# Gating groups taken in pairs, ten feed-forward chunks tile by tile, and norm and mixer steps issued by an account of product time and vector time

## The chip, the cores and the metric

One core of one Trainium2 chip runs the whole kernel. The metric is the device time in microseconds (us) of one execution; the kernel before has a median of 2253.11 us over three runs (2252.66 to 2253.3). Engine names are those of the profile: PE is the matrix engine (PEld its weight loads), DVE the vector engine, ACT the scalar engine, SP the engine whose queue issues the DMAs.

## The reference, cut to what matters

A two-layer encoder step for 1024 prompt rows and 32 sample rows that share weights. Layer 0 mixes by spatial gating, layer 1 by multi-scale pooling. Each layer ends in a squared-ReLU feed-forward part (FFN).

```python
for i in range(DEPTH):                       # DEPTH = 2, D_MODEL = 1024
    sh1, sc1, gt1, sh2, sc2, gt2 = split(silu(c) @ w_ada[i] + b_ada[i])
    h = rmsnorm(x, g_norm[i, 0]) * (1 + sc1) + sh1
    if i == 0:
        z = gelu(h @ w_in); u, v = split(z)  # 2048 columns each, 8 groups of 256
        v = rmsnorm(v, g_v)
        mix = (u * (W_s v + b_s)) @ w_out    # W_s: 128x128 per group, per 128-row chunk
    else:
        mix = (pooled(h, windows 2, 4, 8, 16) - h) @ w_grp * scale
    x = x + gt1 * rmsnorm(mix, g_norm[i, 1])
    h = rmsnorm(x, g_norm[i, 2]) * (1 + sc2) + sh2
    f = square(relu(h @ w_up[i])) @ w_down[i]    # 4096 hidden columns
    x = x + gt2 * rmsnorm(f, g_norm[i, 3])
```

All is float32. The kernel keeps that precision by splitting every product into three: each operand is a rounded high part and a low part, and high x high, high x low and low x high are summed (`products`, L733 to L739).

## The kernel before, in words

**Tiles.** The 1056 rows stand along the free dimension, in three tiles: tile 0 and tile 1 have 384 columns, tile 2 has 256 prompt and 32 sample columns (288). Features stand on the 128 partitions in eight blocks (`KB`). `acc[t]` holds the running sum or x of tile t, `hh[t]` and `hl[t]` the high and low part of the normalised input.

**Stages.** First the start (x in, first norm), then the v half of the gating input (`v_order`, L835), then eight gating groups (`sgu_item`), then FFN of layer 0, the pooling mixer, FFN of layer 1, and the output. FFN runs in eight chunks of 512 hidden columns for each layer. An item, `ffn_item(p, t, after)`, is one chunk for one tile: four `up(j)` of 24 products each and, later, a `down()` of eight output blocks of 12 products each. A gating item has two `up(k)`, each followed by the small spatial products `psp`, and a `down()` of eight blocks of 6 products. Each `down` is put off: it is appended to `pending` and carried out by `flush()` behind the first `up` of the next item.

**Passes.** `passes` (L271 to L274) is the order of FFN work. A wide pass takes a chunk's weights once for all three tiles; a narrow pass (one tile in its list) loads and splits the same chunk's weights again for each tile. Before, chunks 6 and 7 of layer 0 and chunks 0 and 1 of layer 1 are narrow, that is four chunks, and gating groups 6 and 7 are also taken tile by tile. So tile 0 is finished early there, and its norm and mixer work runs beside products of tiles 1 and 2.

**Streams.** `stream` is the order written out by hand in which weight pieces (512 KB each, eight for an FFN chunk) and pieces of `w_ada` come in. `issue()` loads ahead into three raw buffers (`RAW_SLOTS`). `stream_step()` takes the next one: a weight piece is copied to its high part on ACT (L346), and the low part is made on DVE (L347); an ada piece is eight multiply-adds on DVE (L417, L419) and a fold on PE. A weight piece may be split only when the piece eight places before it is done (`stream_ready`).

**Fillers.** Norm and mixer work is written as generators in the deque `fillers`: `residual` (L651), `apply` (L696), `Stat.finish` (L634), the pooling `run` (L1127), the output `run` (L1323), the sample state `sgu_state` (L849). `weave(budget, streams)` (L554) is called behind each `up` and each block of `down`: it takes up to `streams` stream steps, and then pulls filler steps until their written costs (the yielded numbers) have used up a budget fixed for the place: 3.0 behind an FFN `up`, 1.3 behind a block of its `down`. Every third pull goes to the second filler in the deque. `finish(tag)` (L564) pulls all that is left of a filler, at the place where a tile's input is needed.

**Small buffers.** `x3` has three buffers for DMA targets and windows (`t_x`): the gating input `vl`, the rows `vst` and `gvb` of `sgu_state`, the old x `xo` of `residual`, the pooling windows. `pm` has three PSUM buffers (`ps_ms`), for statistics, transposes and, at the end, half of the last tile's transposed output (`last_ps`). The final order of each engine is made by the framework from the recorded program, so it isn't quite the order of the source.

Of the kernel before, what the change touches and what calls it, by code (L numbers as in the profile page):

```python
# [34 lines left out]
def tile_stream_encoder_step(  # L35
# [27 lines left out]
    tt = nc.vector.tensor_tensor  # L63
    stt = nc.vector.scalar_tensor_tensor
    ts = nc.vector.tensor_scalar
    mm = nc.tensor.matmul

# [15 lines left out]

    hs = const.tile([P, KB, 2 * DEC], F32R, name="hs")
# [148 lines left out]
    def w_group(g):  # L233
        for k in range(2):
            f = 2 * g + k
            add_w(
                ("u", g, k),
                sgu_w_in[0][:, f * P : (f + 1) * P].rearrange("(k p) f -> p k f", p=P),
                (8, P),
            )  # L240
        for q in range(2):
            add_w(
                ("o", g, q),
                sgu_w_out[0][g * 256 : (g + 1) * 256, q * 512 : (q + 1) * 512].rearrange(
                    "(k p) d -> p k d", p=P
                ),
                (2, 512),
            )
# [51 lines left out]
    for g in range(8):  # L300
        w_group(g)
        if g > 0:
            some_ada(2)
    some_ada(99)
# [191 lines left out]
    def stream_step():  # L496

        k = state["next"]
        kind, key, ap, shape = stream[k]
        issue()  # L500
        run_deferred()
        r = raws.pop(k)
        if kind == "w":
            do_w(key, r)
        elif kind == "ada":
            (do_ada_pe if k < first_ada else do_ada)(*key, r)
        else:
# [5 lines left out]
        return {"w": 1.1, "ada": 2.6, "x": 1.2}[kind]  # L513
# [22 lines left out]
    turn = [0]  # L536

    def pull():

        if sticky:  # L540
            f = sticky.pop()
        else:
            turn[0] += 1
            f = fillers[1 if turn[0] % 3 == 2 and len(fillers) > 1 else 0]
        try:
            cost = next(f[1])
        except StopIteration:
            fillers.remove(f)
            return 0.0
        if cost < 0:  # L550
            sticky.append(f)
        return abs(cost)

    def weave(budget, streams=1):  # L554
        if streams:
            n = 0
            run_deferred()
            while n < streams and stream_ready():
                budget -= stream_step()
                n += 1  # L560
        while budget > 0 and fillers:
            budget -= pull()

    def finish(tag):  # L564
        while any(f[0] == tag for f in fillers):
            pull()


    def spread(t, ss, tag, out, dg):

        npr, nsm = TILES[t][1], TILES[t][2]
# [9 lines left out]
        yield 0.4  # L581
# [6 lines left out]
        yield 0.1  # L588

    class Stat:  # L590
# [43 lines left out]
        def finish(self, out):  # L634
            n = self.n
            yield 0.5
# [3 lines left out]
            yield 0.3  # L640
# [3 lines left out]
            act(out=q, in_=r, func=AF.Square)  # L644
            stt(out=q, in0=pn[:, :n], scalar=-0.5 / D, in1=q, op0=ALU.mult, op1=ALU.mult)
            stt(out=r, in0=q, scalar=1.5, in1=r, op0=ALU.add, op1=ALU.mult)
            out.append(r)
            yield 2.0


    def residual(st, l, cf, tag, out, store=True, stat=True):  # L651
# [12 lines left out]
        for half in range(2):  # L664
            for k2 in (2 * half, 2 * half + 1):
                load(k2)
            for k2 in (2 * half, 2 * half + 1):
                for k in (2 * k2, 2 * k2 + 1):
# [10 lines left out]
                    yield -0.46  # L679
# [4 lines left out]
                yield 0.9 if k2 % 2 else -0.9  # L684
# [11 lines left out]
    def apply(t, l, cf, sh, r, keep=False):  # L696
        hh[t] = room("h", t, f"hh{l}_{cf}_{t}", F32R)
        hl[t] = room("l", t, f"hl{l}_{cf}_{t}", F32R)
        for k in range(KB):
# [21 lines left out]
            yield 0.95  # L721
# [23 lines left out]
    def v_mm(ps, p, b, ks):  # L745
# [4 lines left out]
        for k in ks:  # L750
            wh, wl = need_w(("v", p, k // 2))
            o = (k % 2) * 512
            if b == 8:
                a = hs[:, k, :]
# [4 lines left out]
                continue  # L759
            a_h = hh[t][:, k, c0 : c0 + m]  # L760
# [57 lines left out]
    nc.vector.tensor_copy(hs[:, :, 0:DEC], hh[NT - 1][:, :, 256 : 256 + DEC])  # L818
    nc.vector.tensor_copy(hs[:, :, DEC:], hl[NT - 1][:, :, 256 : 256 + DEC])
# [18 lines left out]
    for p, b in v_order:  # L838
# [8 lines left out]
        weave(2.0, 1)  # L847

    def sgu_state():  # L849
        for q in range(4):  # L850
# [15 lines left out]
            yield 0.5  # L866
# [10 lines left out]
    def t_hid(kind, name):  # L877
        return work.tile([P, 384], F32R, tag="h" + kind, bufs=5 if kind == "h" else 4, name=name)
# [23 lines left out]
    def sgu_group(g):  # L902
        raw = sgu.tile([P, P], F32, tag="ws", bufs=1, name=f"ws{g}")
        nc.sync.dma_start(raw, sgu_w_s[0, g])
        bb = sgu.tile([P, P], F32, tag="bs", bufs=2, name=f"bs{g}")
# [3 lines left out]
        wt = sgu.tile([P, P], F32, tag="wt", bufs=2, name=f"wt{g}")  # L909
# [4 lines left out]
    def sgu_item(g, t, wt, bb, after):  # L914
# [3 lines left out]
        vl = t_x(f"vl{g}_{t}", [P, 3, 256])  # L918
        nc.sync.dma_start(
            vl[:, :nch, :],  # L920
            vd[col0 : col0 + npr, g * 256 : (g + 1) * 256].rearrange("(c p) d -> p c d", p=P),
        )
        if nsm:
            nc.sync.dma_start(vl[:nsm, nch, :], vd[SEQ : SEQ + nsm, g * 256 : (g + 1) * 256])
        wr = t_m(f"wr{g}_{t}")
        for c in range(nch):
            b = col0 // P + c
            ts(wr[:, c * P : (c + 1) * P], wt, rv[:, b : b + 1], None, op0=ALU.mult)
        if nsm:
            ts(wr[:nsm, npr : npr + nsm], wt[:nsm, :nsm], rv[:nsm, 8:9], None, op0=ALU.mult)  # L930
        hid = []

        def up(k):
            f = 2 * g + k
            ps = ps_up(f"pu{g}_{t}_{k}")
# [5 lines left out]
            sp = ps_up(f"psp{g}_{t}_{k}")  # L941
            for c in range(nch):
# [38 lines left out]
        def down():  # L981
            for d in range(KB):
                ps = ps_dn(f"po{g}_{t}_{d}")
                wh, wl = need_w(("o", g, d // 4))
                terms = []
                for k in range(2):
                    o = k * 512 + (d % 4) * P
                    a, b = hid[k]
                    terms.append((wh[:, o : o + P], wl[:, o : o + P], a[:, :n], b[:, :n]))
                products(ps, n, terms)  # L990
                accumulate(t, d, ps, g == 0)
# [4 lines left out]
                if t == NT - 1 and d % 4 == 3:  # L996
                    w_finish(("o", g, d // 4))
                weave(0.4, d % 2)
            if after is not None:
                after(st)  # L1000

        up(0)
        weave(1.0)
        flush()
        up(1)
        weave(1.0)
        pending.append(down)

    def ffn_item(p, t, after):
# [17 lines left out]
        def down():  # L1027
            for d in range(KB):
# [19 lines left out]
                weave(1.3, d % 2)  # L1048
# [3 lines left out]
        for j in range(4):  # L1052
            up(j)
            weave(3.0)
# [29 lines left out]
    def mix_to_ffn(st, l):  # L1084
# [4 lines left out]
        if l == 1 and t == NT - 1:  # L1089
            for i, (c0, r0, nr) in enumerate(LAST):  # L1090
                for half in range(2):
                    pt = ps_ms(f"xt{i}_{half}")
                    for k in range(4):
# [7 lines left out]
                    yield 0.3  # L1101
# [6 lines left out]
    groups = {}  # L1108
    u_order = [(g, t) for g in range(6) for t in range(NT)]
    u_order += [(g, t) for t in range(NT) for g in (6, 7)]  # L1110
    for g, t in u_order:
        if t == 0:
            groups[g] = sgu_group(g)
        sgu_item(g, t, *groups[g], to_ffn0 if g == 7 else None)
# [7 lines left out]
    def to_pool(st):  # L1122
# [4 lines left out]
        def run():  # L1127
# [7 lines left out]
            if nsm:  # L1135
# [16 lines left out]
                yield 0.5  # L1152
            for k in range(KB):
# [18 lines left out]
                yield 0.5  # L1172
# [4 lines left out]
            yield 0.2  # L1177
            if t == NT - 1:
                for src, out_ap, nm in (
# [3 lines left out]
                    for half in range(2):  # L1183
                        so = t_x(f"stp_{nm}{half}", [P, 512])
                        pt = ps_ms(f"stT_{nm}{half}")
                        for i in range(4):
# [5 lines left out]
                    yield 1.0  # L1192
# [4 lines left out]
            for src, w, dst0, nm in parts:  # L1197
                for g in range(4):
# [3 lines left out]
                    for lev in range(g + 1):  # L1202
# [10 lines left out]
                        yield -0.9  # L1213
# [27 lines left out]
                    yield 1.0 if g == 3 else -1.0  # L1241

            sp = Stat(t, f"rp_{t}")
            for g in range(4):
                if g % 2 == 0:
# [14 lines left out]
                yield 0.3  # L1260
# [16 lines left out]
    def to_out(st):  # L1277
# [8 lines left out]
        def last():  # L1286
# [34 lines left out]
            yield 1.0  # L1321

        def run():  # L1323
# [4 lines left out]
            yield from residual(st, 1, 3, f"r2_1_{t}", [], store=False, stat=False)  # L1328
            for c0, w, dst in blocks:
                yo = t_raw(f"yo{t}_{c0}")  # L1330
# [6 lines left out]
                yield 0.5  # L1337
# [50 lines left out]
```

## Time and profile before

| | |
|---|---|
| profiled execution | 2255.41 us, span 2253.6 us |
| median of three runs | 2253.11 us |
| PE / PEld busy | 2204.2 / 2099.0 us |
| DVE busy | 1302.1 us |
| ACT busy | 863.2 us |
| DMA | 245.31 MB, 109 GB/s on average |
| granted PE clock, mean | 0.992 |

The span runs from the first to the last instruction, and the profiled execution's own time is 1.8 us longer. Busy shares are averages over stages. A stage's table of windows has, for each stretch, the busy time and the number of instructions of each engine, then the granted PE clock (1.00 is full speed), the share of DMA busy time and GB/s.

### The profile page before, as it was taken

The page shows a single profiled execution, that of the slowest core. Times are in us where ns is not written, and L with a number is a line of the kernel's source. Part 1 is how long each engine was busy: PE and PEld are TensorE (multiplying, and loading weights), DVE is VectorE, ACT ScalarE, POOL GpSimd, SP SyncE. Part 2 cuts the span into 40 slices and gives each one's busy share as a digit, 9 for nine tenths or more (in the row PEclk, how much of TensorE's full clock was granted, in tenths as well). Part 3 has the DMA queues.
Part 4 walks back from the last instruction along what each step waited for, and adds up shares of the span by engine and source line. Part 5 has one row for each costly group of instructions (what it writes and reads, how often), then busy time and mean ns, then how long its engine had stood idle before and what let it go on. Part 6 is the DMA issues. An engine that isn't in the chain of part 4 may idle for free.

```text
span 2253.6 us, 33288 instructions
## 1 busy us (share of the span) xinstructions
PE 2204.2 (98%) x13478; PEld 2099.0 (93%) x13478; DVE 1302.1 (58%) x2607; ACT 863.2 (38%) x1549; POOL 0.7 (0%) x6
## 2 busy tenths in 40 slices
PE   7999999999999999999999999899999999999998
PEld 5777899999989999999999999789899999999998
DVE  4855756555698366484664579999752322323345
ACT  4633431122356413223232466666652322313334
POOL 0000000000000000000000000000000000000000
PEclk9999999999999999999999999899999999999999
DMA  8465532122143223232332455564550211202112
GB/s 291 151 224 164 175 100 86 60 69 70 49 136 108 94 85 113 85 122 94 94 103 76 136 157 154 183 189 150 183 168 11 66 38 38 75 10 66 41 50 91
DMA packets 269629, 245.31 MB, mean 109 GB/s; under 512 B 8642, under 2 KB 247690, under 8 KB 269476
## 3 DMA queue, kind: packets, MB, share of 16 engines
q1 hardware_dynamic: 269204, 243.10, 34.4%
q8 instruction: 105, 1.72, 0.3%
q14 instruction: 48, 0.39, 0.1%
q10 hardware_dynamic: 272, 0.10, 0.0%
HBM read 211.32 MB, written 31.84 MB: 108 GB/s over the span
## 4 chain that ended last, share of the span: by engine, by line
PE 89%; DVE 4%; DMA 3%; ACT 2%; issue 1%; SPq 0%; DVEq 0%; ACTq 0%
PE pf L737 11%; PE pg L737 10%; PE pf L738 10%; PE pf L739 10%; PE pg L738 10%; PE pg L739 10%; PE pu L737 3%; PE po L737 3%; PE po L739 2%; PE po L738 2%; PE pu L738 2%; PE pu L739 2%; PE pv L762 2%; PE pv L763 2%; PE pv L764 2%; PE psp L943 1%
## 5 line engine op out<-in xcount | busy, mean ns | idle before, releaser
L737 PE MATMUL pf<-hh,wh_up 128*128 128x384 f32 (+1 forms) x1536 | 499.7, 325 | 4.3 <-ACT hh L712 3.7
L738 PE MATMUL pf<-hl,wh_up 128*128 128x384 f32 (+1 forms) x1536 | 498.8, 325 | 1.1 <-DVE hl L713 1.1
L737 PE MATMUL pg<-fh,wh_dn 128*128 128x384 f32 (+1 forms) x1536 | 497.1, 325 | 2.0 <-ACT fh L881 1.0
L739 PE MATMUL pf<-hh,wl_up 128*128 128x384 f32 (+1 forms) x1536 | 497.3, 324 | 0.0
L738 PE MATMUL pg<-fl,wh_dn 128*128 128x384 f32 (+1 forms) x1536 | 495.7, 323 | 1.2 <-DVE fl L882 1.1
L739 PE MATMUL pg<-fh,wl_dn 128*128 128x384 f32 (+1 forms) x1536 | 495.1, 322 | 0.0
L889 DVE TENSOR_TENSOR acc<-acc,pg 128x384 f32<-128x384 f32 (+1 forms) x336 | 173.8, 518 | 272.0 <-PE pg L739 270.9
L737 PEld LDWEIGHTS pf<-hh,wh_up 128*128 128x128 f32 x1536 | 289.4, 188 | 9.2 <-ACT hh L712 4.4
L737 PEld LDWEIGHTS pg<-fh,wh_dn 128*128 128x128 f32 x1536 | 289.1, 189 | 5.7 <-issue 2.0
L738 PEld LDWEIGHTS pg<-fl,wh_dn 128*128 128x128 f32 x1536 | 289.4, 188 | 2.9 <-DVE fl L882 2.3
L738 PEld LDWEIGHTS pf<-hl,wh_up 128*128 128x128 f32 x1536 | 289.7, 189 | 2.1 <-DVE hl L713 1.5
L739 PEld LDWEIGHTS pf<-hh,wl_up 128*128 128x128 f32 x1536 | 289.6, 189 | 0.2
L739 PEld LDWEIGHTS pg<-fh,wl_dn 128*128 128x128 f32 x1536 | 289.2, 188 | 0.0
L1021 ACT ACTIVATE r<-pf 128x384 f32<-128x384 f32 (+1 forms) x192 | 87.5, 458 | 415.2 <-PE pf L739 410.9
L419 DVE SCALAR_TENSOR_TENSOR aa<-raw,csil,aa 128x256 f32<-128x256 f32 x560 | 231.6, 478 | 3.1 <-DMA raw<-in_w_ada_dram 3.1
L882 DVE TENSOR_TENSOR fl<-r,fh 128x384 fp32r<-128x384 f32 (+1 forms) x192 | 100.2, 522 | 181.8 <-ACT fh L881 166.9
L346 ACT ACTIVATE wh_up<-raw 128x1024 fp32r<-128x1024 f32 x96 | 101.6, 1058 | 264.2 <-PE pf L738 244.1
L347 DVE TENSOR_TENSOR wl_up<-raw,wh_up 128x1024 fp32r<-128x1024 f32 x96 | 117.4, 1223 | 130.2 <-ACT wh_up L346 130.0
L346 ACT ACTIVATE wh_dn<-raw 128x1024 fp32r<-128x1024 f32 x96 | 101.6, 1059 | 121.0 <-PE pg L738 107.9
L347 DVE TENSOR_TENSOR wl_dn<-raw,wh_dn 128x1024 fp32r<-128x1024 f32 x96 | 117.3, 1222 | 46.2 <-ACT wh_dn L346 46.1
L737 PE MATMUL po<-ush,wh_o 128*128 128x384 f32 (+1 forms) x384 | 127.3, 333 | 3.7 <-DVE acc L889 3.5
L737 PE MATMUL pu<-hh,wh_u 128*128 128x384 f32 (+1 forms) x384 | 126.5, 329 | 2.0 <-DVE rv L830 1.6
(262 smaller groups left out, 2949.5 us busy)
## 6 DMA issues: line engine op xcount, KB each, us to landing
raw<-in_w_ada_dram SPq DMA_DIRECT2D x96, 512.0 KB, 3.7
raw<-in_ffn_w_up_dram SPq DMA_DIRECT2D x96, 512.0 KB, 4.2
raw<-in_ffn_w_down_dram SPq DMA_DIRECT2D x96, 512.0 KB, 3.4
raw<-in_sgu_w_in_dram SPq DMA_DIRECT2D x32, 512.0 KB, 4.7
xd<-acc SPq DMA_DIRECT2D x8, 1536.0 KB, 7.0
xo_r<-xd SPq DMA_DIRECT2D x32, 384.0 KB, 4.0
vd<-vt SPq DMA_DIRECT2D x32, 256.0 KB, 3.0
raw<-in_sgu_w_out_dram SPq DMA_DIRECT2D x16, 512.0 KB, 3.5
```

The costliest lines, as they stand in the source:

```text
L346: act(out=wh, in_=r, func=AF.Copy)
L347: tt(out=wl, in0=r, in1=wh.bitcast(F32), op=ALU.subtract)
L419: stt(out=aa[:, v, :], in0=w, scalar=k, in1=aa[:, v, :], op0=ALU.mult, op1=ALU.add)
L737: mm(ps[:, :n], wh, rh, start=i == 0, stop=False)
L738: mm(ps[:, :n], wh, rl, start=False, stop=False)
L739: mm(ps[:, :n], wl, rh, start=False, stop=i == last)
L762: mm(ps[:m, :], a_h, wh[:, o : o + 512], start=k == 0, stop=False)
L763: mm(ps[:m, :], a_h, wl[:, o : o + 512], start=False, stop=False)
L764: mm(ps[:m, :], a_l, wh[:, o : o + 512], start=False, stop=k == KB - 1)
L882: tt(out=dst_lo[:, :n], in0=src[:, :n], in1=dst_hi[:, :n].bitcast(F32), op=ALU.subtract)
L889: tt(out=A(t, d), in0=A(t, d), in1=ps[:, :n], op=ALU.add)
L1021: act(out=r[:, :n], in_=ps[:, :n], func=AF.Relu)
```

## The change

- **Gating groups in pairs.** `sgu_item(gs, t, mix, after)` takes two groups: four `up`, each with its stream step, then one `down` whose eight blocks sum 12 products instead of two times eight blocks of 6. `w_groups` streams the four u pieces of a pair ahead of its four o pieces. All four pairs go over the three tiles in turn. `flush()` stands behind the first of the four. The inputs `vl` and `wr` of the second group are made when its first `up` begins.
- **Passes.** Ten chunks are narrow in place of four: chunks 0, 1 and 4 to 7 of layer 0, and 0 to 3 of layer 1. The ada pieces of layer 1 stand behind the gating pairs and the wide passes.
- **Account.** `tick(us)` adds PE time for every group of products, and wrapped `tt`, `stt` and `ts` add DVE time for every instruction. `weave` pulls fillers while the DVE account is behind the PE account. A yielded number is now a gate (the filler waits until the PE account has passed it), `True` keeps the same filler, `False` gives it up. `finish` pulls by force.
- **Smaller things.** `hs` lives in two `rr` buffers; `bs` and `wt` have three buffers, low parts of hidden tiles five; where a filler of the tile is still there at chunk 0, `flush()` is called ahead of `finish`.

```diff
+    time = {"pe": 0.0, "dve": 0.0}
+    def tick(us):
+        time["pe"] += us
+        time["dve"] = max(time["dve"], time["pe"] - 4.0)
+    def on_dve(op, fixed, rate):
+        def run(out, *args, **kw):
...
+            time["dve"] += fixed + n / rate
+            return op(out, *args, **kw)
+        return run
+    tt = on_dve(nc.vector.tensor_tensor, 0.16, 930.0)
+    stt = on_dve(nc.vector.scalar_tensor_tensor, 0.16, 840.0)
+    ts = on_dve(nc.vector.tensor_scalar, 0.1, 930.0)
...
-    passes = [(0, c, every) for c in range(6)]
-    passes += [(0, c, [t]) for t in every for c in (6, 7)]
-    passes += [(1, c, [t]) for t in every for c in (0, 1)]
-    passes += [(1, c, every) for c in range(2, 8)]
+    passes = [(0, c, [t]) for t in every for c in (0, 1)]
+    passes += [(0, c, every) for c in range(2, 4)]
+    passes += [(0, c, [t]) for t in every for c in range(4, 8)]
+    passes += [(1, c, [t]) for t in every for c in range(4)]
+    passes += [(1, c, every) for c in range(4, 8)]
...
+    groups = [(g, g + 1) for g in range(0, 8, 2)]
+    for i, gs in enumerate(groups):
+        w_groups(gs)
+        if i < 3:
+            some_ada((6, 8, 8)[i])
+    wide = [n for n, (l, _, tiles) in enumerate(passes) if len(tiles) > 1]
     for n in range(len(passes)):
         w_chunk(n)
-        if n > 0:
-            some_ada(10)
+        if n in wide:
+            some_ada(12 if passes[n][0] == 0 else 2)
...
-    def weave(budget, streams=1):
+    def weave(streams=1):
...
-        while budget > 0 and fillers:
-            budget -= pull()
+        while time["dve"] < time["pe"] and fillers:
+            if not pull():
+                break
     def finish(tag):
         while any(f[0] == tag for f in fillers):
-            pull()
+            pull(True)
...
     def products(ps, n, terms):
+        tick(3 * len(terms) * (0.004 + n / 2265.0))
...
-        up(0)
-        weave(1.0)
-        flush()
-        up(1)
-        weave(1.0)
+        for j in range(4):
+            up(gs[j // 2], j % 2)
+            weave()
+            if j == 0:
+                flush()
         pending.append(down)
...
                 if c == 0:
+                    if any(f[0] == f"ffn{l}_{t}" for f in fillers):
+                        flush()
                     finish(f"ffn{l}_{t}")
```

More of the change, by code (lines that the diff above doesn't have):

```diff
@@ L535, in tile_stream_encoder_step, with pull, open_ @@
     sticky = []
-    turn = [0]
-    def pull():
+    gates = {}
+    def pull(force=False):
+        def open_(f):
+            return force or gates.get(f[0], 0.0) <= time["pe"]
         if sticky:
-            f = sticky.pop()
-        else:
-            turn[0] += 1
-            f = fillers[1 if turn[0] % 3 == 2 and len(fillers) > 1 else 0]
+            f = sticky[-1]
+            if not open_(f):
+                return False
+            sticky.pop()
+        else:
+            f = next((f for f in list(fillers)[:2] if open_(f)), None)
+            if f is None:
+                return False
         try:
-            cost = next(f[1])
+            step = next(f[1])
         except StopIteration:
             fillers.remove(f)
-            return 0.0
-        if cost < 0:
+            return True
+        if step is True:
             sticky.append(f)
-        return abs(cost)
-    def weave(budget, streams=1):
+        elif step is not False:
+            gates[f[0]] = max(time["pe"], time["dve"]) + step
+        return True
+    def weave(streams=1):
         if streams:
@@ L587, in spread @@
         out.append(pb)
-        yield 0.1
+        yield False
     class Stat:
@@ L817, in tile_stream_encoder_step @@
         pass
-    nc.vector.tensor_copy(hs[:, :, 0:DEC], hh[NT - 1][:, :, 256 : 256 + DEC])
-    nc.vector.tensor_copy(hs[:, :, DEC:], hl[NT - 1][:, :, 256 : 256 + DEC])
+    hs = []
+    for half in range(2):
+        x = work.tile([P, 384], F32R, tag="rr", bufs=2, name=f"hs{half}")[:, : 8 * DEC].rearrange(
+            "p (k n) -> p k n", k=4
+        )
+        ks = slice(4 * half, 4 * half + 4)
+        nc.vector.tensor_copy(x[:, :, 0:DEC], hh[NT - 1][:, ks, 256 : 256 + DEC])
+        nc.vector.tensor_copy(x[:, :, DEC:], hl[NT - 1][:, ks, 256 : 256 + DEC])
+        hs.append(x)
     rv = const.tile([P, 9], F32, name="rv")
@@ L877, in t_hid @@
     def t_hid(kind, name):
-        return work.tile([P, 384], F32R, tag="h" + kind, bufs=5 if kind == "h" else 4, name=name)
+        return work.tile([P, 384], F32R, tag="h" + kind, bufs=5, name=name)
     def split(dst_hi, dst_lo, src, n):
@@ L908, in sgu_group @@
         nc.tensor.transpose(pt[:, :P], raw, ident)
-        wt = sgu.tile([P, P], F32, tag="wt", bufs=2, name=f"wt{g}")
+        wt = sgu.tile([P, P], F32, tag="wt", bufs=3, name=f"wt{g}")
         nc.vector.tensor_copy(wt, pt[:, :P])
@@ L1106, in to_ffn0 @@
         fillers.append((f"ffn0_{st.t}", mix_to_ffn(st, 0)))
[L1108 to L1114, printed above, removed]
+    for gs in groups:
+        mix = {g: sgu_group(g) for g in gs}
+        for t in range(NT):
+            sgu_item(gs, t, mix, to_ffn0 if gs == groups[-1] else None)
     sgu_stack.close()
```

157 lines of the change are left out of this document (85 added, 72 removed).

## Prediction

> **What bounds the kernel now.** I read the page first, then PE's waits, then a table of windows by stage, then the vector engine's groups by shape.
>
> ```profile
> PE 2204.2 (98%) x13478; PEld 2099.0 (93%) x13478; DVE 1302.1 (58%) x2607; ACT 863.2 (38%) x1549; POOL 0.7 (0%) x6
> PE 89%; DVE 4%; DMA 3%; ACT 2%; issue 1%; SPq 0%; DVEq 0%; ACTq 0%
> ```
>
> PE is busy for 98% of the span, and the change takes no product away. So all that can be won is the time in which PE has nothing to do or runs at a lowered clock. The table by stage shows where that is (columns: stretch, length, busy time and count of PE, PEld, DVE, ACT, POOL, granted clock, DMA share, GB/s):
>
> ```profile
> 230.00:300.00 70.00, 66.73 (x397) 60.19 (x396) 41.99 (x98) 33.87 (x57) 0.00 (x0) 1.00 0.56 169
> 620.00:710.00 90.00, 81.44 (x481) 77.34 (x481) 83.08 (x166) 54.60 (x95) 0.00 (x0) 0.94 0.41 130
> 710.00:1380.00 670.00, 669.91 (x4228) 655.26 (x4227) 403.10 (x808) 236.59 (x413) 0.00 (x0) 1.00 0.34 106
> 1380.00:1500.00 120.00, 109.65 (x632) 99.09 (x631) 109.15 (x173) 78.22 (x140) 0.00 (x0) 0.94 0.57 175
> 1500.00:1590.00 90.00, 90.00 (x521) 87.59 (x520) 82.49 (x151) 58.53 (x103) 0.00 (x0) 1.00 0.60 181
> 1590.00:1660.00 70.00, 66.59 (x424) 61.79 (x423) 49.20 (x100) 46.61 (x92) 0.00 (x0) 1.00 0.55 173
> 2225.00:2253.60 28.60, 19.95 (x154) 18.77 (x152) 16.82 (x34) 13.82 (x34) 0.00 (x0) 0.91 0.31 111
> ```
>
> From 710 to 1380, PE is idle for 0.1 us. Three places lose time. At the border between gating and FFN of layer 0 (620 to 710), idle time is 90 - 81.4 = 8.6 us, and the clock, at 0.94, costs up to 0.06 x 90 = 5.4: **14.0 us**. At the pooling border (1380 to 1500), 10.35 idle and 0.06 x 120 = 7.2 by the clock, then 3.4 idle from 1590 to 1660: **21.0 us**. At the start of the gating stage (230 to 300): **3.3 us**. In the first two, DVE is the busy one: 83.1 of 90 and 109.2 of 120. PE's waits name the same work:
>
> ```profile
> PE pf L737 <- ACT hh L712: 3.7, 1, 3.7
> PE pn_rs L639 <- ACT sc_rs L624: 3.6, 2, 2.2
> PE po L737 <- DVE acc L889: 3.5, 4, 1.3
> ```
>
> PE waits for the next tile's input, for its statistics, and for PSUM blocks that DVE hasn't added yet. That is DVE overload, not a late weight. The stretch 1500 to 1590 is as telling: DVE is busy for 92% of it, and PE for all of it. So at 92% DVE still keeps up.
>
> **Both borders, in DVE work.** Durations (last number before the bar's end is the mean in ns):
>
> ```profile
> L347 DVE TENSOR_TENSOR wl_up<-raw,wh_up 128x1024 fp32r<-128x1024 f32 x96 | 117.4, 1223 | 130.2 <-ACT wh_up L346 130.0
> L889 DVE TENSOR_TENSOR acc<-acc,pg 128x384 f32<-128x384 f32 x224 | 123.3, 552 | 209.2 <-PE pg L739 209.2
> L882 DVE TENSOR_TENSOR fl<-r,fh 128x384 fp32r<-128x384 f32 x128 | 71.1, 555 | 167.7 <-ACT fh L881 166.6 <-PE pg L738 1.0
> L889 DVE TENSOR_TENSOR acc<-acc,po 128x384 f32<-128x384 f32 x112 | 61.3, 551 | 29.8 <-PE po L739 29.7
> L889 DVE TENSOR_TENSOR acc<-acc,po 128x288 f32<-128x288 f32 x56 | 24.0, 449 | 1.4 <-PE po L739 0.8
> L681 DVE TENSOR_TENSOR acc<-acc,xo_r 128x768 f32<-128x768 f32 x32 | 30.4, 951 | 0.0
> L713 DVE SCALAR_TENSOR_TENSOR hl<-acc,mod,hh 128x384 fp32r<-128x384 f32 x32 | 19.0, 612 | 0.4 <-ACT hh L712 0.4
> L671 DVE SCALAR_TENSOR_TENSOR acc<-acc,coef,r_rf 128x384 f32<-128x384 f32 x32 | 18.5, 613 | 0.1
> L612 DVE TENSOR_TENSOR sq_rf<-sq_rf 128x384 f32<-128x384 f32 x28 | 15.6, 557 | 10.3 <-ACT sq_rf L603 10.2
> L616 DVE TENSOR_TENSOR sq_r_0x<-sq_r_0x 128x768 f32<-128x768 f32 x9 | 8.6, 952 | 0.4 <-ACT sq_r_0x L603 0.4
> L1233 DVE SCALAR_TENSOR_TENSOR acc<-win1p,acc 128x768 f32<-128x768 f32 x4 | 3.8, 950 | 0.0
> L1205 DVE TENSOR_TENSOR win0p<-acc 128x798 f32<-128x798 f32 x4 | 3.9, 984 | 0.0
> 1510.00:1520.00 10.00, 10.00 (x59) 10.00 (x59) 10.00 (x14) 7.24 (x12) 0.00 (x0) 1.00 0.82 253
> ```
>
> The last row gives the pace of 384-column products: 10 / 59 = 0.17 us. A narrow FFN item has 192, so 32.6 us, or 24.5 at 288 columns. On DVE it has eight low parts at 1.22, eight additions at 0.55 and four splits at 0.555: 16.4 us; tile 2 some 15.1. One tile's way through the pooling border is two residuals (2 x (8 x 0.613 + 4 x 0.951) = 17.4), four sums of squares (6 x 0.952 + 14 x 0.557 = 13.5), the input's scaling (8 x 0.61 = 4.9), ten window sums (9.8) and four differences (3.8), 16 writes for the next input (9.8) and some ten small steps of the norms at 0.61: 65 us; tile 2, an estimate by its columns, 52.
>
> *Pooling border.* Before, from tile 0's last block in layer 0 to tile 2's first product in layer 1, PE has two chunks each of tiles 1, 2, 0 and 1: 65 + 49 + 65 + 65 = 244 us, pooling products left out. DVE has 33 + 30 + 28 + 28 (in chunk 0 ACT writes the block) for these items and 182 of mixer work: 301 us. Too much, and 21 us are lost. After, there are four chunks each: 488 us of products against 119 + 129 + 182 = 430 on DVE, 88%. That is below the 92% at which PE had no gap. I count 4 us left over (pool statistics that PE still awaits, bursts), between 0 and 12: **-17 us**.
>
> *FFN border of layer 0.* The loss has two halves in the 10 us windows: tile 0's start (640 to 660) and tile 1's (680 to 700).
>
> ```profile
> 640.00:650.00 10.00, 5.38 (x27) 3.75 (x25) 10.00 (x20) 6.21 (x11) 0.00 (x0) 0.88 0.15 39
> 650.00:660.00 10.00, 9.43 (x55) 8.86 (x56) 6.78 (x19) 7.26 (x11) 0.00 (x0) 0.78 0.17 52
> ```
>
> Here 5.2 us are idle, and 0.12 x 10 + 0.22 x 10 = 3.4 go to the clock: 8.6; the other 5.4 of the 14.0 belong to tile 1. Tile 1's start now has one more narrow chunk of tile 0 ahead of it (33 us of products, 16 of DVE work), so I drop that loss. Tile 0's window is as short as before, but paired groups halve the additions in it: for two groups 8 x 0.551 and 8 x 0.449, 8 us less. Still, in the changed kernel's issue order seven of eight `hl` writes and six scalings stand behind the last gating product, with four additions and squares and two weight pieces: 13 x 0.61 + 4 x 0.45 + 2 x 1.22 + 0.6 = 12.8 us of DVE against the first two `up` (48 products, 8.2 us). 4.6, so I take 5 left, between 2 and 9: **-9 us**.
>
> Counted over that whole order at these durations, 25 us of PE work now have at most 26.5 us of DVE work beside them; before, the worst stretches at the two borders have 31 to 35.
>
> **The start of gating: a new wait.** `sgu_state` takes eight `x3` buffers in turn (four `vst`, four `gvb`). Before, its steps were pulled in the first `down`. Now the account pulls all five behind the first three `up`, so the `vl` of group 1 is allocated behind them, and PE's second group of spatial products (`psp1`) waits for it. Prices, columns as in the lists of issues (KB, us to landing):
>
> ```profile
> vst<-vd SPq DMA_DIRECT2D x4, 64.0 KB, 2.7
> gvb<-in_sgu_g_v_dram SPq DMA_DIRECT2D x4, 64.0 KB, 3.4
> out_dram<-vst SPq DMA_DIRECT2D x4, 64.0 KB, 2.9
> vl<-vd SPq DMA_DIRECT2D x16, 384.0 KB, 3.1
> L857 DVE SCALAR_TENSOR_TENSOR vst<-vst,rv,gvb 32x512 f32<-32x512 f32 x4 | 2.9, 736 | 4.2 <-DMA gvb<-in_sgu_g_v_dram 4.1
> L419 DVE SCALAR_TENSOR_TENSOR aa<-raw,csil,aa 128x256 f32<-128x256 f32 x560 | 231.6, 478 | 3.1 <-DMA raw<-in_w_ada_dram 3.1
> ```
>
> With three buffers, from the last read of group 0's `vl`: `vst1` in 2.7, multiply 0.74, out 2.9, `gvb2` in 3.4, multiply 0.74, `vst2` out 2.9 (in SP's queue `gvb3`, which needs that buffer, stands ahead), `vl` 3.1: 16.5 us. PE has the third `up` and 18 products of the `down` to do meanwhile: 42 x 0.17 = 7.1. So 9.4 us idle. Behind the waiting `psp1` on PE's queue stands the whole rest. Lower end: without the wait for `vst2` out, 6.5. Upper end: 16 ada steps (16 x 0.478 = 7.6) stand in DVE's order between two multiplies and cover 6.3 of transfers, and SP's issues add to each step: 12. A stall of 4.6 us in 640 to 650 was followed by 3.4 us lost to a lowered clock; I add 2.5.
>
> The Trainium skill ("TensorE: Matmul & The Clock Gate", Part 1) says that an idle window of about 3.4 us halves the clock until a busy one has passed. By it a 9.4 us stall would add half of one or two such windows, 1.7 to 3.4 us as an estimate, and the sum would be 2236 to 2238; the trace agrees with 0.88 and 0.78 after 4.6 us idle.
>
> The old 3.3 us came from o pieces (needed after two `up`, now after three, 4 us later) and I let them go. Net **+8.5 us**, between +3 and +13.
>
> **The end.** In the changed order, `out_1`'s 24 transposes stand behind the last tile's, and wait for `pm` buffers that the final multiplies read.
>
> ```profile
> 2246.79 4.19 DVE L1312 SCALAR_TENSOR_TENSOR xlast<-yT,r_last,xlast 128x512 f32<-128x512 f32 x6
> 2231.10 2.04 ACT L1335 ACTIVATE yo<-yT 128x512 f32<-128x512 f32 x4
> 2228.63 1.06 PE L1334 MATMUL yT<-ident,acc 128*128 128x128 f32 x8
> ```
>
> The first transposes start after two multiplies (1.4 us), then six copies follow at 0.51, the first two one after the other with four transposes (0.5) ahead of each: about 6 us where the multiplies take 4.2, and two issues and a larger DMA come behind: +3.7. But 24 x 0.13 = 3.1 of PE time leave the stage ahead. Net **+1**, between -1 and +4.
>
> **Costed at nothing.** 96 more weight pieces (50 MB): 117 us of DVE less 64 x 0.551 + 32 x 0.449 = 50 saved, and 96 copies on ACT, all beside PE. They lie in narrow stretches with PE at 100%, counted above.
>
> **The sum.** 2255.4 - 17 - 9 + 8.5 + 1 = 2238.9 for a profiled run. That lies 2.3 above the median of the runs, so **2237 us**.
>
> **Rivals.**
> *B, the start of gating stays covered* (PE gets other products first): then 3.3 is won there in place of 8.5 lost: 2237 - 11.8 = 2225. For: PE has other products of the pair to do, if they stand ahead. Against: in the issue order they stand behind `psp1`. 17%.
> *C, PE binds throughout.* The account keeps DVE full wherever fillers exist, so that waits come back spread over the longer borders; half of what the borders lose stays: -8.5 - 4.5 + 8.5 + 1 = -3.5, 2250. For: 98% PE. Against: the losses are seen with DVE at 91 to 92% and PE idle. The Trainium skill ("Perfetto Trace Analysis", Identifying the Most-Contended Engine) has one improve the engine with the highest occupancy, here PE, which this change leaves as it is; by that alone the time stays at 2253. 13%.
> *D, slower: weights come late in the narrow chunks.*
>
> ```profile
> raw<-in_ffn_w_up_dram SPq DMA_DIRECT2D x96, 512.0 KB, 4.2
> L346 ACT ACTIVATE wh_up<-raw 128x1024 fp32r<-128x1024 f32 x96 | 101.6, 1058 | 264.2 <-PE pf L738 244.1
> ```
>
> A raw buffer is held for 4.2 + 1.06 on ACT + 1.22: with three, a piece each 2.2 us, and tile 2 needs one each 24.5 / 8 = 3.1. It decides from a landing of 7.0 us on. At 8.5 us a piece takes 3.6: ten tile-2 items lose 8 x 0.5 each, 40 us: 2277. Against: four chunks are so now, at 175 to 181 GB/s without a weight wait. 6%.
> *E, the account doesn't issue in time*, steps are forced at `finish`, and the borders lose as before: 2253 + 9.5 = 2263. In the issue order only tile 0's last eight steps in layer 0 are so. 4%.
>
> **How the numbers follow.** My case has 60%; its own range is 2229 to 2246. With every bound at its best (-21, -12, +3, -1) it gives 2222; B lies inside, and C gives 2250. The range is 2222 to 2250; D and E are left out. A measurement can tell about 0.2%, 4.5 us. Faster: my case, B and a little of C, 0.82; same: the rest of C, 0.08; slower 0.10.
>
> **What would show it.** Right: near 230 PE idle for 9 us with `psp` released by the `vl` DMA; the pooling border without idle stretches above 2 us and clock 1.00; DVE near 1370 us. Wrong: raw DMAs as releasers of PE; PE idle for over 10 us between 1100 and 1650; or `pn` waits as long as before.

## The result, and the profile after

The changed kernel takes **2239.57 us** (median of 4 runs, 2238.69 to 2240.11) against 2253.2 before: a ratio of 0.9935, 95% interval 0.9918 to 0.9952. The forecast was 2237. The profiled execution is 2238.69 us, its span 2236.9. The busy times on the page:

```profile
PE 2197.3 (98%) x13478; PEld 2101.8 (94%) x13478; DVE 1371.4 (61%) x2609; ACT 957.5 (43%) x1645; POOL 0.7 (0%) x6
```

PE is idle for 2236.9 - 2197.3 = 39.6 us in place of 49.4, and its busy time is 6.9 us shorter with the same products. Together that is the whole 16.7 us between the spans. In windows of 1 us (busy time x (1 - granted clock), summed), a lowered clock takes 10.0 us of the busy time in place of 12.9; what the other 4 us of shorter busy time come from, the trace doesn't show. The table by stage (columns as in the prediction):

```profile
230.00:300.00 70.00, 58.39 (x328) 52.14 (x327) 43.49 (x102) 25.53 (x42) 0.00 (x0) 0.93 0.54 162
300.00:640.00 340.00, 340.00 (x2191) 331.27 (x2190) 198.89 (x458) 82.04 (x142) 0.00 (x0) 1.00 0.30 92
660.00:690.00 30.00, 25.36 (x147) 22.76 (x146) 24.38 (x51) 21.09 (x34) 0.00 (x0) 0.89 0.36 111
690.00:715.00 25.00, 23.99 (x136) 23.68 (x135) 23.47 (x34) 17.94 (x30) 0.00 (x0) 0.99 0.57 177
715.00:1350.00 635.00, 635.00 (x3874) 625.00 (x3874) 412.27 (x707) 290.37 (x470) 0.00 (x0) 1.00 0.46 140
1350.00:1650.00 300.00, 299.88 (x1865) 292.10 (x1864) 242.69 (x399) 186.51 (x321) 0.00 (x0) 1.00 0.55 168
```

The pooling border, 21.0 us of loss before, has 0.1 us idle left at full clock. The FFN border of layer 0 still loses 4.6 + 1.0 idle and 0.11 x 30 = 3.3 by the clock: 9. The start of gating is now the worst place, 11.6 us idle. PE's five longest waits from 230 us on say why; the sixth row is the longest for a `pn` at the two borders:

```profile
PE psp L997 <- DMA vl<-vd: 5.0, 1, 5.0
PE ada L453 <- DVE aa L79: 4.6, 1, 4.6
PE yT L1393 <- DVE xlast L79: 1.8, 1, 1.8
PE pf L772 <- DVE hl L79: 1.7, 1, 1.7
PE po L771 <- ACT ush L925: 1.5, 1, 1.5
PE pn_r_2x L671 <- ACT xt L1154: 0.3, 1, 0.3
```

The first two lie back to back at 264 to 275, the forecast stall; the last is all that is left of the `pn` waits at the borders.

### The profile page after: what moved, and what is told of

It reads as the page before. It is cut to its first block, busy times and chain, and to the rows that moved or that the text cites. A ratio compares the mean times of both kernels' runs of the same rounds, so it can differ in the third digit from the quotient of the medians.

```text
span 2236.9 us, 33683 instructions
## 1 busy us (share of the span) xinstructions
PE 2197.3 (98%) x13478; PEld 2101.8 (94%) x13478; DVE 1371.4 (61%) x2609; ACT 957.5 (43%) x1645; POOL 0.7 (0%) x6
## 4 chain that ended last, share of the span: by engine, by line
PE 91%; DMA 1%; DVE 1%; ACT 1%; issue 0%; DVEq 0%; SPq 0%; ACTq 0%
PE pf L771 11%; PE pf L772 11%; PE pf L773 11%; PE pg L771 11%; PE pg L772 11%; PE pg L773 11%; PE pu L771 3%; PE po L771 3%; PE po L772 3%; PE po L773 3%; PE pu L772 3%; PE pu L773 3%; PE pv L798 1%; PE pv L799 1%; PE pv L800 1%; PE pp L1310 1%
## 5 line engine op out<-in xcount | busy, mean ns | idle before, releaser
L367 ACT ACTIVATE wh_up<-raw 128x1024 fp32r<-128x1024 f32 x144 | 152.7, 1061 | 287.2 <-PE pf L772 230.8
L79 DVE TENSOR_TENSOR wl_up<-raw,wh_up 128x1024 fp32r<-128x1024 f32 x144 | 176.2, 1224 | 160.8 <-ACT wh_up L367 160.4
L367 ACT ACTIVATE wh_dn<-raw 128x1024 fp32r<-128x1024 f32 x144 | 152.7, 1061 | 206.2 <-PE pg L772 173.3
L79 DVE TENSOR_TENSOR wl_dn<-raw,wh_dn 128x1024 fp32r<-128x1024 f32 x144 | 176.2, 1224 | 86.4 <-ACT wh_dn L367 86.4
```

The costliest lines, as they stand in the source:

```text
L79: return op(out, *args, **kw)
L367: act(out=wh, in_=r, func=AF.Copy)
```

## The experiments

Times are medians of 4 runs (before_n4_ada and both_singles 10), beside the kernel before, whose medians there were 2254.1 to 2254.9.

**1. state_late: the stall at the start of gating.**

```diff
-    fillers.append(("state", sgu_state()))
     for gs in groups:
+        if gs == groups[1]:
+            fillers.append(("state", sgu_state()))
...
-            yield False
+            yield 12.0      # at the end of each step of sgu_state
```

> The changed kernel, but the steps of sgu_state begin with the second pair of groups and come at least 12 us apart by the account. Theory (the three x3 buffers: vl of group 1 waits behind vst and gvb): PE's wait for vl (5.0 us) and the wait for the ada sum ahead of it (4.6 us, DVE held by the vst multiplies) both go, PE idles for about 3 us between 230 and 300 in place of 11.6, and the time falls by 8 to 10 us, to about 2230. Rival 1 (the ada step is late by itself, since DVE still has 16 steps of 0.48 us to do): only the vl wait goes, about 2234.5. Rival 2 (the ring is short wherever these steps stand): the wait comes back in the second pair, 2238 to 2240.

Measured: 2227.29, ratio 0.988 (0.9864 to 0.9897), 12.3 us less than the changed kernel.

```profile
230.00:300.00 70.00, 67.38 (x392) 61.45 (x391) 40.22 (x100) 28.44 (x46) 0.00 (x0) 1.00 0.46 143
```

2.6 us idle in place of 11.6, at full clock. Both waits go, and nothing comes back in the second pair: from 300 to 400 PE is never idle. The wait for the ada sum was no second loss. Its fold ran on PE at 268.59, ahead of the `psp` that needed `vl`, and `vl` itself was late. In the changed kernel SP issued it only when a `vst` had been written out (two issues, then one of SP's waits):

```profile
266.98 0.33 SPq L909 DMA_DIRECT2D out_dram<-vst  x1
270.08 0.38 SPq L968 DMA_DIRECT2D vl<-vd  x1
SPq L968 <- DMA out_dram<-vst: 1.3, 2, 0.7
```

From the last read of group 0's `vl` (256.47) to the `psp` that waited (274.60) it is 18.1 us. The third `vst` multiply, ahead of that write, stood on DVE behind nine ada steps (3.6 us). The order of issue and SP's wait show the three `x3` buffers as the cause; a wider ring was not tried. The rest of the 12.3 is mostly clock: PE's busy time is 2.9 us shorter.

**2. pool_narrow2 and pool_narrow3: a shorter pooling border under the account.**

```diff
-    passes += [(0, c, every) for c in range(2, 4)]
-    passes += [(0, c, [t]) for t in every for c in range(4, 8)]
-    passes += [(1, c, [t]) for t in every for c in range(4)]
-    passes += [(1, c, every) for c in range(4, 8)]
+    passes += [(0, c, every) for c in range(2, 6)]            # three: range(2, 5)
+    passes += [(0, c, [t]) for t in every for c in (6, 7)]    # three: (5, 6, 7)
+    passes += [(1, c, [t]) for t in every for c in (0, 1)]    # three: (0, 1, 2)
+    passes += [(1, c, every) for c in range(2, 8)]            # three: range(3, 8)
```

> The changed kernel with the account, the pairs and layer 0's chunks 0 and 1 as they are, but only two chunks tile by tile on each side of the pooling border (chunks 6 and 7 of layer 0, 0 and 1 of layer 1), as in the kernel before. Theory (DVE had 301 us of work for 244 us of products; only the length of the border helps): the loss of about 20 us comes back, 2255 to 2261, with over 10 us of PE idle at the border. Rival (the account spreads the steps, length is not needed): 2240 to 2244, PE idle under 3 us there.

> The changed kernel with three chunks tile by tile on each side of the pooling border (5 to 7 of layer 0, 0 to 2 of layer 1). By the prediction's count: 366 us of products beside 182 + 186 = 368 us of DVE work. Theory (DVE work against products decides, and what doesn't fit is forced at finish without cover): at 100% a part of the steps is forced; between pool_narrow2 (301 for 244, 118 us lost) and the changed kernel (430 for 488, nothing lost), nearer to the latter: 2255 to 2285. Rival (the account needs only a little length, three chunks are enough): 2238 to 2243.

Measured: two chunks on each side 2357.87 (ratio to before 1.046, 1.0445 to 1.0476), three chunks 2281.34 (1.0119, 1.0104 to 1.0134). Two lose 118 us against the changed kernel, more than five times the 21.0 that the kernel before loses here, and far more than theory or rival said; three lie inside the theory's range. Windows and PE's two longest waits of pool_narrow2, then windows of pool_narrow3:

```profile
1425.00:1500.00 75.00, 51.21 (x257) 44.07 (x256) 47.07 (x75) 39.35 (x69) 0.00 (x0) 0.82 0.39 121
1525.00:1610.00 85.00, 49.02 (x209) 39.84 (x209) 76.42 (x127) 39.54 (x65) 0.00 (x0) 0.76 0.43 135
1650.00:1750.00 100.00, 67.89 (x356) 58.16 (x355) 66.65 (x150) 47.36 (x100) 0.00 (x0) 0.80 0.35 111
```

```profile
PE pn_r_1x L671 <- ACT sc_r_1x L656: 17.4, 2, 15.9
PE pn_r_0x L671 <- ACT sc_r_0x L656: 15.0, 1, 15.0
```

```profile
1350.00:1500.00 150.00, 140.09 (x889) 133.10 (x889) 124.44 (x188) 93.98 (x160) 0.00 (x0) 0.97 0.57 171
1500.00:1600.00 100.00, 86.84 (x447) 79.78 (x446) 73.30 (x130) 52.69 (x88) 0.00 (x0) 0.90 0.48 147
1600.00:1720.00 120.00, 113.26 (x634) 108.86 (x633) 78.12 (x146) 65.52 (x120) 0.00 (x0) 0.97 0.48 148
```

There is one gap ahead of each tile's first product of layer 1, and in two of the three DVE isn't full either (47 of 75, 67 of 100). What the account hasn't issued is forced by `finish` in one piece, with no products beside it: in the order as built, 183 pulls of filler steps at this border with two chunks, 52 with three, none with four. The kernel before, counted in the same way, forces 45 there; its budgets had issued the others earlier. The forced steps wait for one another, PE among them for 15 us at a time. Length is needed, and the account makes a lack of it dear.

**3. before_narrow4 and before_n4_ada: length without the account.** The passes of layer 0's chunks 4 to 7 and layer 1's 0 to 3 one tile at a time, in the kernel before; in the second also the ada pieces moved:

```diff
-        if n > 0:
-            some_ada(10)
+        if n < 4:          # before_n4_ada only
+            some_ada(12)
```

> The kernel before with nothing changed but its list of passes: four chunks tile by tile on each side of the pooling border, no account, no pairs. Theory (length alone removes the DVE overload): 2253.2 - 17 to 21 = 2232 to 2236. Rival (fixed budgets pull the steps too early or too late, the account is needed): half or more of the loss stays, 2243 to 2253. If the 32 narrow passes cost anything of their own (weights, DVE), it shows here as a time above 2236 without idle time at the border.

> The kernel before with four chunks tile by tile on each side of the pooling border, as in before_narrow4, but the 48 ada pieces of layer 1 lie behind the four wide chunks (12 each) in place of 10 behind every pass. Theory (length alone is worth about 14 us; the 22 us lost from 1050 to 1150 in before_narrow4 were ada steps crowded into one-tile passes): 2253.2 - 14.5 = 2238 to 2240, no PE idle above 1 us between 1050 and 1150, some 6 us left at 1450 to 1520. Rival (one-tile chunks cost DVE time that fixed budgets don't see): 2250 or more.

Measured: 2269.8 (1.007, 1.0055 to 1.0085) and 2255.66 (1.0005, 0.9996 to 1.0015): neither theory's number. Windows of before_narrow4 (three rows) and of before_n4_ada (three):

```profile
1040.00:1180.00 140.00, 124.50 (x727) 116.20 (x727) 106.55 (x217) 50.33 (x76) 0.00 (x0) 0.93 0.55 170
1400.00:1560.00 160.00, 154.17 (x985) 145.68 (x984) 144.74 (x248) 105.17 (x185) 0.00 (x0) 1.00 0.62 185
1560.00:1660.00 100.00, 99.61 (x567) 96.82 (x566) 65.17 (x122) 55.06 (x99) 0.00 (x0) 1.00 0.52 158
```

```profile
620.00:700.00 80.00, 70.17 (x421) 65.80 (x420) 74.40 (x150) 45.49 (x78) 0.00 (x0) 0.94 0.43 142
700.00:780.00 80.00, 75.23 (x466) 70.57 (x465) 66.32 (x167) 37.87 (x81) 0.00 (x0) 0.98 0.43 131
1350.00:1650.00 300.00, 291.62 (x1792) 280.09 (x1791) 240.73 (x418) 181.64 (x320) 0.00 (x0) 0.98 0.56 168
```

In before_narrow4 ten ada pieces still follow each pass, now also the one-tile passes: 15.5 us idle and up to 0.07 x 140 = 9.8 by the clock at 1040 to 1180. In before_n4_ada that is gone, but 12 pieces follow the first pass: from 620 to 780 it loses 14.6 idle and up to 6.4 by the clock, where the kernel before loses 14.0. At the pooling border 6.2 us are left in the first. In the second it is 8.4 idle from 1350 to 1650 and up to 0.02 x 300 = 6 by the clock, 14 of 21.0. So length alone saves 7 to 15 us there, not all, and what before_n4_ada saves there it loses at 620 to 780.

Over these 300 us its DVE share is 240.7 / 300 = 80%; the changed kernel has 242.7 / 300 = 81% and no gap. Why, no run separates. The account doesn't spread the steps more evenly: in windows of 10 us from 1400 to 1560, DVE's share runs from 52 to 100% in before_n4_ada and from 36 to 100% in the changed kernel. What differs is which steps are issued when, and also a fifth buffer for the low parts of hidden tiles.

**4. no_flush: the FFN border of layer 0.** The `flush()` ahead of `finish` in `run_ffn`, and the `if` around it, are taken out.

> The changed kernel without the flush ahead of finish: the last tile's down products of gating go behind the first up of FFN layer 0, as in the kernel before. Theory (the down products cover the 12.8 us of DVE steps that are forced there): without them PE waits longer for hl, 3 to 8 us slower, 2243 to 2248. Rival (the flush itself exposes the last hidden block's chain, some 4 us between 660 and 675): 2 to 4 us faster, 2236 to 2238.

Measured: 2232.83, ratio 0.9904 (0.989 to 0.9919): 6.7 us faster than the changed kernel, against the theory and by more than the rival said. Rows of the changed kernel in 5 us windows, then one of no_flush:

```profile
660.00:665.00 5.00, 4.18 (x20) 3.31 (x19) 4.05 (x11) 4.92 (x7) 0.00 (x0) 0.82 0.26 85
670.00:675.00 5.00, 3.22 (x22) 2.69 (x21) 4.87 (x12) 3.47 (x7) 0.00 (x0) 1.00 0.76 236
680.00:685.00 5.00, 3.84 (x27) 3.52 (x25) 4.59 (x9) 3.17 (x6) 0.00 (x0) 1.00 0.57 175
685.00:690.00 5.00, 4.12 (x14) 3.40 (x15) 5.00 (x10) 2.98 (x5) 0.00 (x0) 0.71 0.38 109
```

```profile
660.00:690.00 30.00, 28.44 (x185) 27.59 (x184) 23.77 (x49) 20.47 (x33) 0.00 (x0) 0.94 0.31 94
```

The first two rows are the last gating tile, where PE waits for `wr` (0.6) and for the chain of the last hidden block (`po` for `ush`, 1.5). The other two are tile 0's first products, which wait for `hl` (1.7). Without the flush, the first `up` of FFN goes among the `down` products, and PE has work while `hl` is made: the waits for `hl`, `r` and `wr` are gone. The one for `ush` stays at 1.5 and is the 1.6 us idle that are left, so the flush isn't its cause; the rival had taken it for that.

**5. both: 1 and 4 together.**

> The changed kernel with the edits of state_late and of no_flush together. Theory (the two losses lie at different places, 250 to 275 and 660 to 690, and add up): 2239.6 - 12.3 - 6.8 = 2220 to 2221. Rival (the clock or DVE's order at the second place depends on the first): 2223 to 2227.

Measured: 2219.31, ratio 0.9845 (0.983 to 0.986). The two add up. The next kernels differ from this one.

**6. both_singles: groups one by one.**

```diff
-    groups = [(g, g + 1) for g in range(0, 8, 2)]
+    groups = [(g,) for g in range(8)]
-        if i < 3:
-            some_ada((6, 8, 8)[i])
+        if i in (1, 3, 5):
+            some_ada((6, 8, 8)[i // 2])
-        for j in range(4):
+        for j in range(2 * len(gs)):
```

> As both, but gating groups one by one in place of pairs (twice the down items and additions in gating, half the products in each). Theory (pairs relieve DVE at the border to FFN 0 by 8 us of additions and give the tiles longer items): 4 to 8 us slower than both, with PE waiting for hl or pn between 640 and 700. Rival (account and narrow chunks do it, pairs are worth nothing): within 1.5 us of both.

Measured: 2255.23, ratio to before 1.0003 (0.9993 to 1.0013): 36 us slower than both. Three rows of both_singles, two of both:

```profile
300.00:550.00 250.00, 245.53 (x1566) 235.40 (x1565) 174.89 (x401) 47.93 (x84) 0.00 (x0) 1.00 0.32 102
640.00:700.00 60.00, 49.43 (x273) 46.85 (x272) 53.89 (x104) 34.08 (x59) 0.00 (x0) 0.86 0.30 97
700.00:800.00 100.00, 92.96 (x523) 91.90 (x522) 69.66 (x107) 59.32 (x97) 0.00 (x0) 0.97 0.54 168
```

```profile
640.00:700.00 60.00, 58.17 (x370) 56.63 (x370) 47.46 (x84) 44.54 (x72) 0.00 (x0) 1.00 0.49 148
700.00:800.00 100.00, 100.00 (x582) 99.50 (x581) 77.19 (x137) 62.95 (x109) 0.00 (x0) 1.00 0.59 181
```

The losses are 4.5 in gating, 10.6 + 8.4 up to 700, and 7.0 + 3.0 up to 800, with DVE busy for 90% from 640 to 700. Between 300 and 800, PE waits most for additions and for `ush`:

```profile
PE pg L771 <- DVE acc L79: 7.0, 1, 7.0
PE po L771 <- ACT ush L924: 4.7, 3, 3.2
```

At the border to FFN `finish` forces 57 pulls, and 25 in the kernel both. So pairs are worth far more than theory and rival said, and than the 8 us of additions that I counted. How much of the 36 is forced steps, no run separates.

**7. both_narrow1: one narrow chunk at the start of FFN layer 0.** Chunk 1 of layer 0 goes over all tiles.

> As both, but only chunk 0 of FFN layer 0 goes tile by tile (chunk 1 goes over all tiles). Theory (the second one-tile chunk covers the norm steps of tiles 1 and 2; without it 27 steps of each are forced, 16 us of DVE work each with no products beside it): 15 to 35 us slower than both, 2235 to 2255, with PE idle ahead of the first products of tiles 1 and 2. Rival (the prediction's price for tile 1's half of this border, 5.4): 2224 to 2226.

Measured: 2237.64, ratio to before 0.9925 (0.991 to 0.9939): 18.3 us slower than both. That is in the theory's range. Its windows, and its largest wait there:

```profile
690.00:730.00 40.00, 32.82 (x173) 31.48 (x172) 31.07 (x45) 25.52 (x41) 0.00 (x0) 0.87 0.56 163
730.00:790.00 60.00, 55.04 (x345) 53.53 (x344) 43.05 (x91) 36.61 (x72) 0.00 (x0) 0.94 0.53 160
```

```profile
PE pf L771 <- ACT hh L745: 8.9, 2, 5.4
```

The starts of tiles 1 and 2 wait for `hh`, as at the shortened pooling border; 27 pulls are forced ahead of each.

**8. both_gates_open: the account without its gates.** `open_` always returns true.

> As both, but the account's gates (a step waits until the product time has passed the moment at which its input should be there) are always open. Theory (the gates keep DVE from waiting in order for PE and ACT results of the norms): DVE stalls at pn and statistics, 3 to 10 us slower, 2222 to 2229. Rival (the account of times alone is enough, the gates only delay steps, 12 + 11 forced ones against 6): the same or up to 4 us faster, 2215 to 2219.

Measured: 2218.05, ratio to before 0.9838 (0.9822 to 0.9855), 1.3 us less than both, within what a run varies. No gain of the gates is seen in the total. The trace has two sides: with open gates PE has no idle time from 640 to 700 (1.8 us in the kernel both), but 2.3 us from 1350 to 1650 (0.4 there).

**9. both_lead and both_lead2: the account runs DVE ahead at two places.**

```diff
-        while time["dve"] < time["pe"] and fillers:
+        while time["dve"] < time["pe"] + lead[0] and fillers:   # open_ likewise
...
+                if l == 1 and c == 7 and t == NT - 1:
+                    lead[0] = 6.0
...
+            if gs == groups[-1] and t > 0:      # both_lead2 only;
+                lead[0] = 3.0                   # 0 again behind finish
```

> As both, but in the very last item (tile 2, chunk 7 of layer 1) the account may run DVE 6 us ahead, so that out_1's transposes are issued before the last products and none is forced at the end. Theory (the forced transposes wait for blocks held by the last multiplies and put two DMA issues behind them: 5.9 us longer from the last product to the end, 24 transposes of 0.13 us less before it): the end comes 2.5 to 3.5 us earlier, 2217 to 2218. Rival (DVE is full there, so the earlier steps hold back the last additions by as much): within 1 us of both.

> As both_lead, and besides the account may run DVE 3 us ahead from tile 1's item of the last pair of groups until tile 0's FFN starts, so that the first up of FFN layer 0 comes before the last hidden block of gating is needed. Theory (the 3 to 4 us left between 650 and 690 are the chain of that last hidden block, which then has 24 products beside it): 2213 to 2214.5. Rival (DVE is full there, so that running ahead delays the gating blocks): 2217 to 2220.

Measured: 2216.96 (0.9835, 0.9821 to 0.985) and **2213.86 (0.982, 0.9806 to 0.9835)**, the fastest. First the end of the changed kernel: on PE (start, duration), a window, its last multiplies on DVE and its last copy on ACT. Then the multiplies of both_lead, then two windows of both_lead2:

```profile
2205.40 0.30 PE L773 MATMUL pf<-hh,wl_up 128*128 128x288 f32 x1
2225.60 1.12 PE L1393 MATMUL yT<-ident,acc 128*128 128x128 f32 x4 [1.76 <-DVE xlast L79]
2227.41 4.53 PE L1393 MATMUL yT<-ident,acc 128*128 128x128 f32 x20 [0.69 <-ACT yo L1394]
```

```profile
2225.00:2232.00 7.00, 5.64 (x24) 4.84 (x24) 3.30 (x5) 3.02 (x6) 0.00 (x0) 0.50 0.63 242
2224.14 4.19 DVE L79 SCALAR_TENSOR_TENSOR xlast<-yT,r_last,xlast 128x512 f32<-128x512 f32 x6
2231.97 0.60 ACT L1394 ACTIVATE yo<-yT 128x512 f32<-128x512 f32 x1 [0.26 <-PE yT L1393]
```

```profile
2209.23 4.19 DVE L79 SCALAR_TENSOR_TENSOR xlast<-yT,r_last,xlast 128x512 f32<-128x512 f32 x6
```

```profile
640.00:660.00 20.00, 19.32 (x134) 18.34 (x133) 16.18 (x34) 13.73 (x21) 0.00 (x0) 1.00 0.38 113
660.00:700.00 40.00, 40.00 (x247) 40.00 (x247) 33.52 (x51) 27.93 (x47) 0.00 (x0) 1.00 0.70 212
```

In the changed kernel 24 transposes of `out_1` begin 1.5 us after the multiplies do, the last 20 at 0.23 us each, at a clock of 0.50. In both_lead the multiplies begin at 2209.23 of 2216.0, 6.8 us before the end; in the changed kernel at 2224.14 of 2236.9, 12.8 before it. In both_lead2 the border of layer 0 has 0.7 us idle left, and the wait for `ush` is gone.

## Why the prediction was right, and where it was not

The total holds: forecast -16.5 for the profiled run, measured -16.7; by the medians it is -13.6, where -16.2 was forecast. The terms were off in both directions, so that the total fits this well is partly luck.

| term | forecast | measured |
|---|---|---|
| pooling border | -17 | -21 |
| FFN border, layer 0 | -9 | -5 |
| start of gating | +8.5 | +10 to +11 |
| end | +1 | +3 |

They make -12 to -13, with a lowered clock counted over whole windows, as in the prediction. Counted only while PE is busy, in windows of 1 us, they are -19, -4, +10 and +3, so -9. Another 3 are gone before 230, most of it by the clock, which takes 1.5 to 4.6 us there from run to run; 1 is idle time gone between 300 and 620; and the 4 us of busy time named above I could not place.

*Pooling border: the number nearly, the reason only half.* I priced length alone, as DVE work against products (430 for 488), and gave the account nothing. Length alone leaves 6 to 14 us, and the account at the old length loses 118 (experiments 2 and 3). My residual of 4 became 0.1; at nearly the same DVE share before_n4_ada still lost 14, and why is open. What the sum lacked is what happens to a step that doesn't fit. In the kernel before, 57 us too much DVE work (by my count) forced 45 pulls and cost 21. Under the account the same 57 forced 183 and cost 118, and a surplus of 2 us forced 52 and cost 42. Rival E had that mechanism and a price of 9.5; it isn't met at this border, since with four chunks nothing is forced.

*FFN border: the step that failed is "I take 5 left".* Tile 0's start costs about what I said (680 to 700: 3.0 idle and 1.5 by the clock), and tile 1's loss is gone as said. What I left out is 4 us ahead of it, the waits for `wr` and `ush` in the last gating tile with the clock that they cost. The `flush()`, an edit of the diff that my sum does not name, makes tile 0's start as dear as it is; the `ush` wait stays without it, and is gone in both_gates_open and both_lead2. The second narrow chunk is worth more than the 5.4 us that I took back: without it the starts of tiles 1 and 2 lose 18 us together (both_narrow1).

*Start of gating: right in mechanism and size.* From the last read of `vl` to the next `psp` I forecast 16.5 us, 9.4 of it idle; measured are 18.1 and 4.6 + 5.0 = 9.6. For the clock I added 2.5; it takes 2.0 of the busy time in this stretch, and PE's whole busy time is 2.9 shorter in state_late. By the Trainium skill ("TensorE: Matmul & The Clock Gate", Part 1) the prediction's estimate was 1.7 to 3.4 there, and the 2.0 agrees. Rival B's 2225 is about what state_late reached, by another way: 2227.

*End: mis-sized.* From the last `up` product to the end it is 31.5 us in place of 28.4 (2225.19 to 2253.6 before). The 3.1 us of 24 transposes did leave the stage ahead. The term that failed is the +3.7 behind: from the first of the last multiplies to the end it is 12.8 us in place of 6.8, so +6.0. I let the copies end 6 us after that start; the last ends at 8.4, since the transposes took 0.23 us each at a clock of 0.50 where I had 0.13.

*Costed at nothing:* DVE is at 1371, as forecast, and from 230 us on PE waits for no weight DMA, so D did not happen. C did not either: PE's share of busy time is still 98%, and the time fell by 14 us and, in both_lead2, by 40.

## What to carry to other kernels

An engine that is busy for 98% can still give 40 us if what is lost lies at a few borders; find them by a table of windows, and look there for the engine that feeds it. Before work is issued by an account of times, add up per border what must fit: what doesn't fit is forced at the end without cover, and here it cost far more than its own duration. A step pulled earlier takes its buffers earlier too: count the ring that it shares, not only its engine.

## What was not expected of the hardware

Short stalls can cost clock. In the changed kernel PE idles for 0.8 us between 660 and 663, and the clock is then halved for 3.4 us (0.60 and 0.70 are 0.8 and 0.6 us at half):

```profile
660.00:661.00 1.00, 0.42 (x3) 0.20 (x2) 1.00 (x4) 0.98 (x2) 0.00 (x0) 1.00 0.08 30
663.00:664.00 1.00, 0.99 (x5) 0.99 (x6) 0.66 (x3) 0.97 (x3) 0.00 (x0) 0.60 0.22 51
664.00:665.00 1.00, 1.00 (x6) 1.00 (x6) 0.45 (x1) 1.00 (x1) 0.00 (x0) 0.50 0.97 342
665.00:666.00 1.00, 1.00 (x6) 1.00 (x6) 0.00 (x0) 0.99 (x3) 0.00 (x0) 0.50 0.44 148
666.00:667.00 1.00, 1.00 (x7) 1.00 (x6) 0.46 (x1) 0.09 (x1) 0.00 (x0) 0.70 0.00 0
```

In no_flush a 1.5 us wait for `ush` does the same (0.94 over 30 us). In the kernel both, and in the changed kernel itself at 671, the same wait of 1.5 us leaves the clock at 1.00. So what a stall of this size costs depends on more than its length; on what, no run here separates. The Trainium skill's page named above has the clock halved after an idle window of some 3.4 us that runs freely; idle stretches of a quarter to a half of that were enough here.
